# Modulation rows on VectorE from the third group on, in a two-layer hybrid backbone on one Trainium2 core

## The chip, the core and the metric

The kernel runs on one core of a Trainium2 chip. Time is device microseconds (us) of one launch. The profile follows one execution; its engines are called PE or TensorE (matrix products; PEld is its weight load), DVE or VectorE, ACT or ScalarE, POOL or GpSimd, and SP, whose queue issues nearly all transfers from DRAM here. The on-chip memories are SBUF and, for TensorE's results, PSUM.

## The reference

Two layers over 256 latent tokens and 256 context tokens, width 2048, in float32. Cut to what matters here:

```python
for l in range(DEPTH):                                  # DEPTH = 2
    shift, scale, gate = split(silu(c) @ ada_w[l] + ada_b[l], 3)         # and the same with c_ctx
    h  = rmsnorm(x,  norm_g[l]) * (1.0 + scale)   + shift                # modulation
    hc = rmsnorm(xc, norm_g[l]) * (1.0 + scale_c) + shift_c
    q, k, v, up, uf, g = split_proj(h @ w_in[l])        # and the same of hc
    q = rope(rmsnorm(q, q_norm_g[l])); k = rope(rmsnorm(k, k_norm_g[l]))
    att = softmax attention of q over context and latent keys
    out = (concat(att, pool(up), fourier(uf)) * silu(g)) @ w_out[l]
    x = x + gate * out
return rmsnorm(x, final_norm_g)
```

`silu(c) @ ada_w` is a product of two vectors (c and c_ctx) with a 2048 x 6144 matrix in each layer. The parts shift and scale of layer 0, 2048 x 4096 values, have to be there before the first h is.

## The kernel before, in words

Tokens lie along the free axis and channels on the 128 partitions: x is 16 tiles (k = 0 to 15) of 128 channels x 512 tokens, latent and context side by side, held in four SBUF tiles `xk[0..3]` of four k each. The framework that the kernel is written in places waits and buffers by itself: a tile drawn from a pool with so many buffers waits until an earlier tile of it is free. Instructions of each engine, and the transfers on SP's queue, run in order; the order is made ahead of time from priorities and a model of durations. In the startup TensorE's order is the one written in the code (`manual_schedule`, L989).

Every product with large weights is done in a split form: a float32 value is taken apart into a high and a low part (`split`, L137: ScalarE casts, VectorE subtracts), and three passes (high x high, high x low, low x high) are summed in PSUM.

**The startup** (`startup`, L838 to L1055) does four things at once:

- *The norm.* `stats(g)` (L855) squares the four k of one x tile on ScalarE and VectorE and sums them over partitions by a matmul with a matrix of ones (L871). `norm()` (L875) does the last of them, `stats(3)`, then root and reciprocal (L878, L880).
- *The modulation of layer 0.* It goes by ten groups of k, `GROUPS = (1, 1, 2, 2, 2, 2, 2, 2, 1, 1)`. Group j needs shift and scale for its one or two k: 2048 rows of the matrix by 256 or 512 columns, loaded in four pieces of 512 rows (`piece`, L972; 512 KB or 1 MB; the tile is called `a` in the profile, from pool `st` with four buffers). `ada_part` (L979) multiplies one piece by silu(c) and silu(c_ctx): four matmuls on four column strips of the array. After the last piece the sum is copied (L1018), transposed (L1024), reduced (L1031), biased and scaled (L1039, L1040), and `make_h` (L245) makes the h of its k: a product with the norm's reciprocal (L248), scale and shift (L255), split.
- *A quarter of the rows on VectorE.* `ND[j] = 1` gives one of a group's four pieces to VectorE, so that TensorE has three. `dvec` (L952) loads that piece with columns on the partitions and 512 rows along the free axis, and takes for each of c and c_ctx a product with a copy of silu(c) on all partitions and its sum (L965, eight of them for a group of two k). The copies, `cq`, are read from DRAM (L958), where `late["store"]` (L160) put silu(c) after a transpose in group 0. The partial sums are added at L1038. Before the change the groups 5 to 9 are done like this. `dvec(j + 1)` is called in group j, ahead of its last piece.
- *The first matmuls with h.* Weights `wb` (two column blocks) and `wgs` (some gate columns) are loaded and split as jobs (`queue`, L941), and their matmuls go into a list `backlog`; `work(n)` (L924) takes up to n of them, 14 after each piece of a group of two k. An entry is held back until a counter of pieces, `now`, has reached its `ready` value: the h of group j is taken from the second piece of group j + 1 on (`QK = 1`). With fewer TensorE pieces in a group the counter starts the group further on (`kk + 4 - npc`, L1005).

`warm(n)` (L985) issues n small matmuls of ones into a PSUM tile that is not read.

**Loads in program order.** The first 12 k of x (L832), then in group 0 its first piece, the last four k of x (L999), and the other pieces. SP's queue works through this order; a transfer whose buffer is not free, or whose source is not written, holds up those behind it.

**The layers** follow: column blocks of the input projection (`b_chunk`), with small work put between by a side list, `Side` (L258): each entry has a generator, a delay on the list's own clock (a row of main matmuls counts 0.64) and an entry that it must follow. `q_prep` (L518) makes the queries: norm, rotation, and transposes on TensorE (L525); it is put on the list at L648 with a delay of `LAG_E` = 5.6. Meanwhile VectorE works off the rest of the modulation matrix (L188).

Of the kernel before, what the change touches and what calls it, by code (L numbers as in the profile page):

```python
# [20 lines left out]
P = 128  # L21
# [9 lines left out]
AHEAD = 400  # L31
ST = 4
KS = 8
ND = (0, 0, 0, 0, 0, 1, 1, 1, 1, 1)
KG = 4
NE = 3
DLOW = -60
# [9 lines left out]
LAG_S, LAG_T, LAG_E, LAG_Q = 4.3, 1.4, 5.6, 0.0  # L47
GROUPS = (1, 1, 2, 2, 2, 2, 2, 2, 1, 1)
# [8 lines left out]
def backbone(  # L57
# [24 lines left out]
    V, S, G, PE = nc.vector, nc.scalar, nc.gpsimd, nc.tensor  # L82
# [31 lines left out]
    def load_x(g, n):  # L114
        for j in range(0, 4, n):
            nc.sync.dma_start(xk[g][:, j : j + n], xT[:, 4 * g + j : 4 * g + j + n])

    idt = const.tile([P, P], F32, name="idt")
    ones = const.tile([P, P], F32, name="ones")
# [164 lines left out]
    side = Side()  # L284
# [233 lines left out]
    def q_prep(qraw, qT, rq):  # L518
        rq.append(head_rstd(qraw, 4, P ** -0.5))
        for tt, r in qraw:  # L520
            qo = rope_one(tt, r, 4, 0)
            yield 0.0, 3.0 if tt == 0 else 1.0
            tp = smt()
            for hh in range(4):
                PE.transpose(tp[:, hh * P : hh * P + P], qo[:, hh], idt)  # L525
            c = slice(tt * P, tt * P + P)
            split(tp.rearrange("p (h n) -> p h n", h=4), qT[0][:, :, c], qT[1][:, :, c])
            yield 0.43, 0.0
# [47 lines left out]
    def layer(l, h, xs, chunk0):  # L576
# [62 lines left out]
        for g in range(2):  # L639
            accs = b_chunk(l, 3 + g, h, ntt, FILL[l][2])  # L640
            qraw = evac_raw(accs)
            if l == 0:
                side.finish("a0")
                qT = pair8(4, (T,))
            else:
                qT = [a.rearrange("p a (b n) -> p (a b) n", b=2) for a in pair8(2, (2 * N,))]
            rq = []
            side.add(f"q{g}", q_prep(qraw, qT, rq), LAG_E, "k")  # L648
            for qt in range(ntt):
                side.add(f"a{g}", attention(g, qt, qT, rq, kT, vv, mixed, off), 0.0, f"q{g}")  # L650
        korder = list(range(8, 16)) + list(range(8))
# [48 lines left out]
        k = KT - 1  # L700
# [128 lines left out]
            V.scalar_tensor_tensor(th, th, 1.0, g, op0=ALU.add, op1=ALU.mult)  # L829
        return th  # L830

    for g in range(3):  # L832
        load_x(g, 2)
    cq = [f4("cq", (P, 2, 512), F32) for _ in range(2)]
    h0 = H(T, "h")

# [1 line left out]
    def startup():  # L838
        st = tc.tile_pool(name="st", bufs=ST)
        with st as st:  # L840
# [111 lines left out]
            def dvec(j):  # L952
                gs, k0, n = GROUPS[j], sum(GROUPS[:j]), P * GROUPS[j] * 1024
                for e in range(ND[j]):
                    if ND[j - 1] < ND[j] and not used[e]:
                        used[e] = True
                        for v in range(2):
                            nc.sync.dma_start(cq[e][:, v], late["cd"][v, 1536 - 512 * e : 2048 - 512 * e].partition_broadcast(P))  # L958
                    raw = st.tile([P, 2 * gs, 512], F32, tag="a0", name=name("a0"))
                    pi = start[j] + (3 - e) * n  # L960
                    nc.sync.dma_start(raw, ada0[pi : pi + n].rearrange("(p b r) -> p b r", b=2 * gs, r=512))
                    with tc.high_priority(offset=DLOW):
                        for q in range(2 * gs):
                            for v in range(2):
                                V.scalar_tensor_tensor(  # L965
                                    t2("junk") if v == 0 else raw[:, q], raw[:, q], 1.0, cq[e][:, v], op0=ALU.mult, op1=ALU.mult,
                                    accum_out=abq[:, e, q // gs, k0 + q % gs, v : v + 1],
                                )
# [15 lines left out]

            def warm(n):  # L985
                for _ in range(n):
                    PE.matmul(first[3][:, :P], ones, ones, start=True, stop=True)

            with tc.manual_schedule(engines={mybir.EngineType.PE}):  # L989
                for g in range(3):  # L990
                    stats(g)
                for j, gs in enumerate(GROUPS):
                    a = smt()
                    w_ = 256 * gs
                    npc = 4 - ND[j]
                    raws = []
                    for kk in range(npc):
                        if j == 0 and kk == 1:
                            load_x(3, 1)  # L999
                        if j == 1 and kk == 3:  # L1000
                            late["store"]()
                        if kk == npc - 1 and j + 1 < len(GROUPS):
                            dvec(j + 1)
                        raws.append(piece(j, kk))
                        now[0] = 4 * j + kk + 4 - npc  # L1005
                        if kk + 4 - npc == (PFK if j else 3):
                            queue(4 * j + 4 + (QK if j else Q0), k0, gs)
                        if j == 0 and kk == 2:
                            norm()
                        if j == 0 and kk == 3:  # L1010
                            nc.sync.dma_start(idt, ident)
                        ada_part(a, raws[kk], kk, kk == 0, kk == npc - 1, w_)
                        if j == 1 and kk < 2:
                            warm(3 - 2 * kk)
                        work(RATE * gs // 2)
# [167 lines left out]
```

## Time and profile before

| | |
|---|---|
| median of 3 runs | 1073.24 us (1071.56 to 1074.11) |
| the profiled execution | 1073.19 us, span 1071.4 us |
| TensorE busy | 1047.4 us, 98% of the span |
| VectorE busy | 842.3 us, 79% |
| ScalarE busy | 479.7 us, 45% |
| read from DRAM | 230.58 MB |

The span is the part of the execution that the profile covers. Busy time is summed over an engine's instructions. The "chain of waits" follows the run back from its end, at each step to what released it. A row of instructions gives start, length, engine, line, operation, the tiles written and read, and in square brackets how long the engine had idled before and what ended it. A row of a transfer gives the tiles, the issuing queue, the size, and the time from issue to landing.

### The profile page before, as it was taken

To read this page: it belongs to the slowest core of one execution; us is meant where nothing else is said; L and a number is where in the kernel's file an instruction comes from. 1 tells how busy PE (TensorE), PEld (TensorE's weight loads), DVE (VectorE), ACT (ScalarE), POOL (GpSimd) and SP (SyncE) were. 2 spreads that over 40 slices of the span, in tenths; PEclk is the share of its full clock that TensorE was granted. 3 is DMA by queue.
4 is the path that set the end of the run, shared out by engine and by line. 5 is a ranking of instruction groups with operands and counts; after the bars stand their busy time and mean duration, and the time that the engine had idled before them with its cause. 6 is when DMAs were issued, how large, how long until landed. Compare 5 with 4: busy or idle time off the path is not lost.

```text
span 1071.4 us, 14049 instructions
## 1 busy us (share of the span) xinstructions
PE 1047.4 (98%) x5100; PEld 842.6 (79%) x5100; DVE 842.3 (79%) x1553; ACT 479.7 (45%) x803; POOL 0.2 (0%) x4
## 2 busy tenths in 40 slices
PE   6899999999999999999999999999999999999996
PEld 4466677888787888888888888887888888888885
DVE  6358648998999779998989787489657889776565
ACT  5233225323323766632522223288326767447453
POOL 0000000000000000000000000000000000000000
PEclk9999999999999999999999999999999999999999
DMA  8999777566785244457776667445764565686563
GB/s 336 410 398 343 256 238 242 164 198 214 227 260 169 80 140 158 157 192 273 266 272 213 197 195 265 139 133 169 271 218 161 168 196 185 224 270 212 192 201 117
DMA packets 63797, 233.63 MB, mean 218 GB/s; under 512 B 7104, under 2 KB 8176, under 8 KB 60016
## 3 DMA queue, kind: packets, MB, share of 16 engines
q1 hardware_dynamic: 63152, 231.69, 63.8%
q10 hardware_dynamic: 576, 1.05, 0.3%
q8 instruction: 40, 0.66, 0.3%
q14 instruction: 29, 0.24, 0.1%
HBM read 230.58 MB, written 2.12 MB: 217 GB/s over the span
## 4 chain that ended last, share of the span: by engine, by line
PE 81%; DVE 7%; DMA 4%; ACT 3%; issue 3%; SPq 0%; DVEq 0%; ACTq 0%
PE mm L336 18%; PE mm L335 18%; PE mm L337 18%; PE mm L932 6%; PE mm L311 5%; PE sm L932 3%; DVE ajunk L188 2%; DMA a<-in_ada 2%; PE mm L312 2%; PE sm L336 2%; PE sm L337 2%; PE sm L335 2%; PE sm L981 2%; DVE wlo L139 2%; PE sm L562 1%
## 5 line engine op out<-in xcount | busy, mean ns | idle before, releaser
L138 ACT CAST whi<-raw 128x1024 fp32r<-128x1024 f32 (+1 forms) x216 | 219.9, 1019 | 333.0 <-PE mm L336 112.1
L139 DVE TENSOR_TENSOR wlo<-raw,whi 128x1024 fp32r<-128x1024 f32 (+1 forms) x216 | 255.3, 1182 | 103.7 <-ACT whi L138 102.6
L188 DVE SCALAR_TENSOR_TENSOR ajunk<-araw,cbt 128x1024 bf16<-128x1024 f32 x224 | 273.6, 1221 | 49.8 <-DMA araw<-in_adar 36.9
L335 PE MATMUL mm<-whi,h 128*128 128x512 f32 x416 | 167.6, 403 | 0.0
L336 PE MATMUL mm<-wlo,h 128*128 128x512 f32 x416 | 163.3, 393 | 0.0
L337 PE MATMUL mm<-whi,h 128*128 128x512 f32 x416 | 163.1, 392 | 0.0
L335 PE MATMUL mm<-m,whi 128*128 128x512 f32 (+1 forms) x272 | 102.6, 377 | 0.0
L336 PE MATMUL mm<-m,whi 128*128 128x512 f32 (+1 forms) x272 | 102.4, 377 | 0.0
L337 PE MATMUL mm<-m,wlo 128*128 128x512 f32 (+1 forms) x272 | 102.4, 377 | 0.0
L311 PE MATMUL mm<-h,whi 128*128 128x512 f32 x256 | 92.5, 400 | 0.0
L337 PEld LDWEIGHTS mm<-whi,h 128*128 128x128 f32 x416 | 78.1, 188 | 17.0 <-DVE h L139 0.3
L336 PEld LDWEIGHTS mm<-wlo,h 128*128 128x128 f32 x416 | 78.2, 188 | 16.2 <-issue 1.9
L335 PEld LDWEIGHTS mm<-whi,h 128*128 128x128 f32 x416 | 78.2, 188 | 16.1 <-issue 1.7
L335 PE MATMUL mm<-h,whi 128*128 128x512 f32 x196 | 77.7, 396 | 0.0
L337 PE MATMUL mm<-h,wlo 128*128 128x512 f32 x196 | 76.8, 392 | 0.0
L336 PE MATMUL mm<-h,whi 128*128 128x512 f32 x196 | 76.8, 392 | 0.0
L312 PE MATMUL mm<-h,wlo 128*128 128x256 f32 x256 | 72.4, 283 | 0.0
L932 PE MATMUL mm<-whi,h 128*128 128x512 f32 x192 | 63.8, 401 | 0.2 <-ACT h L138 0.2
L335 PEld LDWEIGHTS mm<-m,whi 128*128 128x128 f32 x272 | 51.2, 188 | 9.5
L337 PEld LDWEIGHTS mm<-m,wlo 128*128 128x128 f32 x272 | 51.2, 188 | 9.4
L336 PEld LDWEIGHTS mm<-m,whi 128*128 128x128 f32 x272 | 51.2, 188 | 9.2
L311 PEld LDWEIGHTS mm<-h,whi 128*128 128x128 f32 x256 | 48.1, 188 | 10.8
(229 smaller groups left out, 1639.1 us busy)
## 6 DMA issues: line engine op xcount, KB each, us to landing
araw<-in_adar SPq DMA_DIRECT2D x128, 512.0 KB, 4.0
raw<-in_wb SPq DMA_DIRECT2D x78, 512.0 KB, 3.6
raw<-in_wg SPq DMA_DIRECT2D x55, 512.0 KB, 4.3
a<-in_ada SPq DMA_DIRECT2D x24, 1024.0 KB, 9.1
raw<-in_wo SPq DMA_DIRECT2D x32, 512.0 KB, 4.3
raw<-in_wot SPq DMA_DIRECT2D x32, 512.0 KB, 3.9
a<-in_ada SPq DMA_DIRECT2D x16, 512.0 KB, 4.6
x<-in_xT SPq DMA_DIRECT2D x4, 1024.0 KB, 8.1
```

The lines of the kernel that those rows point to most:

```text
L138: i = S.copy(hi, src)
L139: V.tensor_sub(lo, src, hi.bitcast(F32))
L188: V.scalar_tensor_tensor(junk, raw, 1.0, cbt[:, v], op0=ALU.mult, op1=ALU.mult, accum_out=acc[:, u, h, v : v + 1])
L311: PE.matmul(a.rearrange("p (s n) -> p s n", s=2), hi[:, j - j0], h.both[k][:, :, :N], start=s0, stop=False)
L312: PE.matmul(a[:, :N], lo[:, j - j0], h.hi[k][:, :N], start=False, stop=s1)
L335: PE.matmul(o, ah, bh, start=start, stop=False)
L336: PE.matmul(o, ah, bl, start=False, stop=False)
L337: PE.matmul(o, al, bh, start=False, stop=stop)
L562: PE.transpose(tp[:, h * P : h * P + P], ps[h][:, i * P : i * P + P], idt)
L932: PE.matmul(o, lt, r, start=s0, stop=s1)
L981: PE.matmul(a[32 * i : 32 * i + 32, :w_], cs[:, 4 * kk + i], raw[:, i], start=first_, stop=last, tile_position=(0, 32 * i))
```

## The change

VectorE gets a quarter of the rows in groups 2, 3 and 4 as well. In these groups `dvec` is called in the group itself, after its first piece; from group 5 on it is called in the group before, as it was, but after that group's last piece has been issued, not ahead of it. The store of silu(c) now comes behind the last piece of group 1. All four tiles of x are loaded ahead of the modulation, and the norm stands ahead of group 0 in TensorE's order. Small matmuls of ones are added at the start and between the pieces of group 0, and they write another PSUM tile. In layer 0 `q_prep` gets 1.5 more delay on the side list.

```diff
-ND = (0, 0, 0, 0, 0, 1, 1, 1, 1, 1)
+ND = (0, 0, 1, 1, 1, 1, 1, 1, 1, 1)
...
-            side.add(f"q{g}", q_prep(qraw, qT, rq), LAG_E, "k")
+            side.add(f"q{g}", q_prep(qraw, qT, rq), LAG_E + (1.5 if l == 0 else 0.0), "k")
...
-    for g in range(3):
-        load_x(g, 2)
+    for g in range(4):
+        load_x(g, 2 if g < 3 else 1)
...
-                    if ND[j - 1] < ND[j] and not used[e]:
+                    if not used[e]:
...
-                    PE.matmul(first[3][:, :P], ones, ones, start=True, stop=True)
+                    PE.matmul(gfirst[0][:, :P], ones, ones, start=True, stop=True)
...
             with tc.manual_schedule(engines={mybir.EngineType.PE}):
+                warm(10)
                 for g in range(3):
                     stats(g)
+                norm()
...
                     for kk in range(npc):
-                        if j == 0 and kk == 1:
-                            load_x(3, 1)
+                        raws.append(piece(j, kk))
                         if j == 1 and kk == 3:
                             late["store"]()
-                        if kk == npc - 1 and j + 1 < len(GROUPS):
+                        if kk == 0 and ND[j] and j < 5:
+                            dvec(j)
+                        if kk == npc - 1 and 5 <= j + 1 < len(GROUPS):
                             dvec(j + 1)
-                        raws.append(piece(j, kk))
                         now[0] = 4 * j + kk + 4 - npc
...
-                        if j == 0 and kk == 2:
-                            norm()
...
                         ada_part(a, raws[kk], kk, kk == 0, kk == npc - 1, w_)
+                        if j == 0 and kk < 3:
+                            warm(2)
```

## The prediction

> **What bounds the kernel now.** I read the page first, then the startup in stretches of 10 us, then the chain of waits in order of time, and last single rows.
>
> ```profile
> span 1071.4 us, 14049 instructions
> PE 1047.4 (98%) x5100; PEld 842.6 (79%) x5100; DVE 842.3 (79%) x1553; ACT 479.7 (45%) x803; POOL 0.2 (0%) x4
> ...
> 20.00:30.00 10.00, 9.51 (x76) 5.59 (x68) 7.00 (x16) 3.52 (x8) 0.00 (x0) 1.00 0.87 311
> 30.00:40.00 10.00, 8.77 (x52) 4.75 (x49) 3.10 (x8) 2.76 (x4) 0.00 (x0) 1.00 1.01 423
> 40.00:50.00 10.00, 7.78 (x45) 3.88 (x45) 6.80 (x14) 2.66 (x5) 0.00 (x0) 1.00 1.02 417
> 50.00:60.00 10.00, 10.00 (x51) 6.41 (x50) 2.16 (x3) 2.78 (x5) 0.00 (x0) 1.00 1.02 417
> ```
>
> The columns after the stretch are its length, then busy us and instructions of PE, PEld, DVE, ACT and POOL, the granted clock, the DMA share and GB/s. Over the whole run TensorE is the bound: 24 us of 1071.4 are not busy. The change lies in the startup, and there the picture has two halves. From 30 to 50 us TensorE has holes while the DMA engines are full (423 and 417 GB/s, share above 1.0). From 50 us TensorE is full and the DMA is nearly so. VectorE has room throughout (3.10 to 6.80 us of 10).
>
> ```profile
> 26.66 7.67 DMA a<-in_ada
> ...
> 34.38 1.11 PE sm L981 x8
> ...
> 35.50 11.06 DMA a<-in_ada
> ...
> 46.61 1.06 PE sm L981 x8
> 47.67 3.40 PE mm L932 x14
> 51.07 1.00 PE sm L981 x8
> ...
> 55.47 1.00 PE sm L981 x8
> ```
>
> This is the chain of waits: start, length, what. Up to 46.6 us it is modulation pieces on their way in; after that only TensorE. So an edit that takes TensorE work out before about 46 us buys nothing by itself, and one that takes it out later buys its full length, as long as the transfers still arrive. They only just do:
>
> ```profile
> a<-in_ada SPq DMA_DIRECT2D x1, 1024.0 KB, 12.3
> ...
> 42.73 0.33 SPq L976 DMA_DIRECT2D a<-in_ada  x1
> ```
>
> The fourth piece of group 3 (counting from 0) is issued at 42.73 us and lands 12.3 us later, at 55.0; its matmuls start at about 55.4. The DMA stream is therefore the bound up to 55 us, with 0.4 us to spare.
>
> **The change, part by part.** *A piece less on TensorE in groups 2, 3 and 4.* A modulation piece of 128x512 takes 1.00 us in the chain (51.07), and 14 main matmuls follow it (3.40 us). The three pieces are worth 3 x 1.0 = 3.0 us of TensorE. Group 2 is used up at 32 to 43 us and group 3 up to 55.4 us, both while the transfers are the bound; only group 4's piece lies wholly in the full stretch. I count **-1.0 us** (bounds 0 and -3.0).
>
> *The same rows on VectorE.* Each group adds eight products.
>
> ```profile
> 73.15 0.69 DVE L965 SCALAR_TENSOR_TENSOR junk<-a,cq 128x512 f32<-128x512 f32 x1
> ...
> 77.44 0.69 DVE L965 SCALAR_TENSOR_TENSOR a<-a,cq 128x512 f32<-128x512 f32 x1
> 78.05 0.08 DVE L965 DVE_READ_ACCUMULATOR a<-a,cq 128x1 f32 x1
> 78.05 1.29 DVE L248 TENSOR_TENSOR xn<-x,rstd 128x512 f32<-128x512 f32 x2
> ```
>
> Eight take 78.05 - 73.15 = 4.9 us; three groups 14.7 us, plus three additions of the partial sum (about 0.2 us each). VectorE idles 6.9 us of 30 to 40 and 7.8 us of 50 to 60, so I cost them at nothing. The cover is the time until the last piece of the same group has landed: the VectorE piece lands ahead of two more pieces, each 1 MB, which at 417 GB/s take 2.5 us each, so 5 us against 4.9 us, and evacuation, transposes and reduction come after. If the products were late by 2 us in one group, the next main matmuls would be late by as much. VectorE is in order: behind a product that waits for its piece stand the splits of the weights, the reduction and the h of the group before, and TensorE's main matmuls wait for these. TensorE has about 3 us to spare between 32 and 43 us; I take 0, bounds 0 and +2.
>
> *The copies of c come forward.* Two loads of 256 KB move from 56.9 us to a place between group 2's first and second pieces, into the stretch that the transfers bound.
>
> ```profile
> 56.88 0.91 SPq L958 DMA_DIRECT2D cq<-cd  x2
> ...
> cq<-cd SPq DMA_DIRECT2D x2, 256.0 KB, 10.6
> ```
>
> 0.52 MB at 417 GB/s is **+1.3 us** on all that lands after them. They also wait for the store of c to DRAM, on SP's in-order queue. Behind them stand the VectorE piece, the weight loads and pieces 1 and 2 of group 2.
>
> ```profile
> 24.34 0.38 SPq L160 DMA_DIRECT2D cd<-crow  x1
> 24.77 2.96 SPq L976 DMA_DIRECT2D a<-in_ada  x4
> ...
> cd<-crow SPq DMA_DIRECT2D x1, 16.0 KB, 2.9
> ...
> a<-in_ada SPq DMA_DIRECT2D x1, 512.0 KB, 4.6
> ```
>
> The store landed in 2.9 us on an almost empty queue; a piece issued just after it took 4.6 us. It now goes out after group 1's last piece, at about 25.2 us, so it lands at 28 to 30. Until then group 1's last piece and group 2's first are under way, 1.5 MB or 3.6 us at 417 GB/s. I take no hole, bounds 0 and +6 (the slower rival below). [...]
>
> *x ahead, and the norm ahead of group 0.* The four loads of x's last quarter move past one 512 KB piece, 1.3 us at 417 GB/s. They feed the squares, and those the reciprocals:
>
> ```profile
> 13.52 1.99 ACT L862 ACTIVATE sq<-x 128x512 f32<-128x512 f32 x3 [1.40 <-DVE sq L868]
> ...
> 19.04 3.37 DVE L880 RECIPROCAL rstd<-rstd 128x256 f32<-128x256 f32 x2 [2.05 <-ACT rstd L878]
> ...
> 22.32 0.11 DVE L1031 TENSOR_REDUCE red<-sm 128x4 f32<-128x16 f32 x1
> ...
> 23.16 0.68 DVE L139 TENSOR_TENSOR wlo<-raw,whi 128x512 fp32r<-128x512 f32 x1
> ...
> 20.29 0.94 PE L987 MATMUL mm<-ones 128*128 128x128 f32 x6
> ...
> 20.37 0.43 SPq L145 DMA_DIRECT2D raw<-in_wb  x1
> ...
> 23.91 0.33 SPq L145 DMA_DIRECT2D raw<-in_wgs  x1
> ```
>
> Both reciprocals end at 22.4 us, together with group 0's reduction, which does not move (the same bytes lie ahead of its last piece). But the first weight split stands behind them on VectorE and ends at 23.84; SP waits for it from 20.8 to 23.91, and that hole is the 311 GB/s of 20 to 30 us. ScalarE's squares of the last quarter waited 1.4 us for buffers that VectorE's additions free, and start no sooner, so I let the reciprocals, the split and SP move by 0.8 us of the 1.3: **-0.8 us** on the stream (bounds 0 and -1.3). The ten plus six small warm matmuls (three took 0.94 us at 20.29, two instructions to a matmul) fill TensorE's holes ahead of 24 us and cost nothing: the ten come before the first squares. Without that cover, ten would cost 3.1 us.
>
> *Order.* With three TensorE pieces, the counter that releases a group's main matmuls is one step further on, so group 1's and group 2's h come up after one piece of the next group, not two, and TensorE waits for h there. The rows I followed it by:
>
> ```profile
> 41.60 1.06 PE L981 MATMUL sm<-a,cs 128*32 128x512 f32 x8
> ...
> 44.13 0.19 DVE L1031 TENSOR_REDUCE red<-sm 128x8 f32<-128x32 f32 x1 [1.53 <-PE sm L1024]
> ...
> 46.17 1.34 DVE L139 TENSOR_TENSOR h<-xn,h 128x512 fp32r<-128x512 f32 x2
> ```
>
> The last piece of group 2, used at 41.6 us now, comes at 41.6 + 1.3 - 0.8 + 0.9 = 43.0 us (two weight loads, 0.9 MB, now stand ahead of it; 0.9 is my allowance for them), its reduction 2.5 us later at 45.5 as now, and the first of the two h 2.7 us after that (46.17 + 0.67 - 44.13), so the first main matmul at 48.2, fourteen of them to 51.6, piece 1 to 52.6, fourteen to 56.0. The last TensorE piece of group 3 lands at 55.0 + 1.3 - 0.8 = 55.5, so I put its start near 55.7, about halfway between what the transfers and what this order allow; it is at 55.4 now: **+0.3 us** net for everything before it (it holds the +1.3 and the -0.8).
>
> *A later start of the q preparation in layer 0*, by 1.5 us of the side queue's clock:
>
> ```profile
> 334.84 0.39 PE L337 MATMUL mm<-whi,h 128*128 128x512 f32 x1
> 336.23 0.63 PE L525 MATMUL sm<-idt,qo 128*128 128x128 f32 x4 [1.00 <-DVE nt L235]
> ```
>
> TensorE stands 1.0 us at the first transposes, waiting for VectorE. Three rounds of 0.64 us later that is gone if VectorE's chain ends when it did: **-1.0 us** (bounds 0, if the chain slips along, and -1.0).
>
> **Sum.** +0.3 - 1.0 - 1.0 = -1.7 us. The span goes to 1069.7 us; the profiled execution took 1073.19 us with 1.8 us outside its span and lies on the median of 1073.24, so I forecast 1073.2 - 1.7 = 1071.5 us.
>
> **The rivals.** *TensorE gets all of it.* If the stream has more slack than I give it (the lost hole at 20 to 30 us closes wholly, and 0.4 us spare was no limit), three pieces, the start and the q wait pay: -3.0 - 0.8 - 1.0 = -4.8, **1068.4 us**. For it: TensorE is the only engine in the chain from 46.6 us. Against it: 417 GB/s and a share of 1.02 up to 60 us.
>
> *Nothing moves.* The transfers eat the pieces (last landing +1.3, no gain at the start) and the q chain slips along: +1.3 - 1.0 = +0.3, **1073.5 us**. For it: the bounds of each term; against it: the waits named above have a releaser that does move.
>
> *Slower: SP stands at the copies of c.* If the store is overtaken by nothing and lands as late as a transfer does once the queue is full:
>
> ```profile
> 27.78 0.54 SPq L145 DMA_DIRECT2D raw<-in_wb  x1
> ...
> raw<-in_wb SPq DMA_DIRECT2D x1, 512.0 KB, 10.4
> ```
>
> 10.4 us, then SP is held from 25.6 to 35.6 us, what is under way runs dry at about 31, and the stream loses 4.6 us: -1.7 + 4.6 = +2.9, **1076.1 us**. It decides from a landing of about 7.5 us, at which the hole outweighs the gains. For it: the stream is the bound just there. Against it: what lies ahead of the store then is little (2.9 us now).
>
> **How the numbers follow.** Less than 0.2%, 2.1 us, can't be told from no change here. The forecast gets 0.45; its own range is 1069.8 to 1073.0, and as 1071.1 us is the mark for faster I give 0.18 of it to faster and 0.27 to no change. TensorE gets all of it: 0.24, faster. Nothing moves: 0.13, no change. Slower: 0.18. So faster 0.42, same 0.40, slower 0.18. The range reaches a little below the second case and nearly to the slower one: 1067.3 to 1075.5.
>
> **What would show it.** In the profile after: 24 more products at L965, first between 34 and 42 us, without a wait of VectorE for a piece ahead of them; matmuls at L981 fewer by 3 x 8; the copies of c issued before 30 us, and a DMA rate above 400 GB/s from 28 to 55 us, which shows the slower rival wrong; the last TensorE piece of group 3 at 55 to 56 us (clearly sooner would show the first rival right); both reciprocals over by 21.7 us; no 1 us wait ahead of the first L525 transposes; the last L932 matmul about 0.7 us sooner than now. The prediction is wrong if TensorE's holes before 50 us shrink by several us, or if SP stands at L958 for over 7 us.

## The result, and the profile after

The changed kernel takes 1078.74 us (median of 6 runs, 1077.86 to 1079.26), the kernel before 1073.28 us beside it (6 runs, 1071.56 to 1074.11). The ratio is 1.0054, 95% interval 1.0041 to 1.0066: slower by 5.5 us, 7.2 us above the forecast and outside its range. The profiled execution took 1078.32 us.

First the page of the changed kernel, then its row for 28 to 34 us and its stretches of 10 us, with the columns of the same view of before.

```profile
span 1076.5 us, 14126 instructions
...
PE 1053.6 (98%) x5108; PEld 847.6 (79%) x5108; DVE 857.3 (80%) x1604; ACT 479.8 (45%) x803; POOL 0.2 (0%) x4
...
28.00:34.00 6.00, 5.67 (x38) 3.23 (x41) 2.25 (x6) 1.16 (x3) 0.00 (x0) 1.00 0.68 233
...
30.00:40.00 10.00, 8.24 (x43) 4.66 (x41) 3.23 (x9) 1.50 (x3) 0.00 (x0) 1.00 0.78 308
40.00:50.00 10.00, 6.95 (x25) 2.78 (x26) 8.05 (x20) 2.42 (x3) 0.00 (x0) 0.66 1.02 412
50.00:60.00 10.00, 8.69 (x45) 5.10 (x44) 9.17 (x27) 1.98 (x3) 0.00 (x0) 1.00 1.03 415
```

The same 6 us of before:

```profile
28.00:34.00 6.00, 4.88 (x30) 2.42 (x29) 2.40 (x7) 1.32 (x3) 0.00 (x0) 1.00 1.01 421
```

The bound stretch has lost transfers. From 28 to 34 us the DMA engines moved 233 GB/s at a share of 0.68, where before moved 421 GB/s at 1.01; over 30 to 40 us it is 308 against 423. The stretches behind it run at 412 and 415 GB/s again (before: 417 in both), so what was lost there is not made up. The granted clock, 1.00 throughout this part of before, is 0.66 from 40 to 50 us.

Where the 5.1 us of span lie is read from the row of the startup's last matmuls, and from the first matmul of layer 0's output projection. The last two numbers of a row are the starts of its first and last instruction; before first, then after.

```profile
L932 PE MATMUL sm<-h,wlo x60: 388/389/499, 30.0 to 170.2; 128*128 128x512 f32 x60
...
L336 PE MATMUL mm<-m,whi x272: 280/389/389, 527.5 to 702.6; 128*128 128x512 f32 x120, 128*128 128x256 f32 x16
```

```profile
L932 PE MATMUL sm<-h,wlo x60: 388/389/796, 31.3 to 175.4; 128*128 128x512 f32 x60
...
L336 PE MATMUL mm<-m,whi x272: 280/389/389, 533.8 to 708.9; 128*128 128x512 f32 x120, 128*128 128x256 f32 x16
```

The startup ends 5.2 us later (175.4 against 170.2) and layer 0 as far as its output projection takes 1.1 us more (533.8 - 175.4 = 358.4 against 357.3). All that follows gives back 1.2 us, so the loss stands in the two places that the change touches. "Startup end" below is the last number of this L932 row.

The chain of waits of the changed kernel, and SP's queue as it worked through the same time (start, length, what):

```profile
24.97 4.60 DMA cd<-crow
30.96 11.33 DMA a<-in_ada
42.33 1.93 PE sm L981 x8
44.27 3.29 PE sm L932 x7
47.55 1.56 PE sm L981 x8
```

```profile
24.97 0.42 SPq L160 DMA_DIRECT2D cd<-crow  x1
25.48 0.37 SPq L976 DMA_DIRECT2D a<-in_ada  x1
29.59 0.80 SPq L958 DMA_DIRECT2D cq<-cd  x2
30.48 0.38 SPq L961 DMA_DIRECT2D a<-in_ada  x1
30.96 0.38 SPq L976 DMA_DIRECT2D a<-in_ada  x1
31.43 1.10 SPq L145 DMA_DIRECT2D raw<-in_wb  x1
32.62 1.61 SPq L145 DMA_DIRECT2D raw<-in_wgs  x1
34.28 1.13 SPq L976 DMA_DIRECT2D a<-in_ada  x2
```

The store of c to DRAM landed after 4.60 us, and SP issued nothing from 25.85 to 29.59 us, when it could issue the copies of c. Group 2's second TensorE piece follows at 30.96 and takes 11.33 us to land. TensorE's own rows (in brackets the idle time before and what ended it) show the price, and VectorE's show that it waited too:

```profile
42.33 1.93 PE L981 MATMUL sm<-a,cs 128*32 128x512 f32 x8 [3.01 <-DMA a<-in_ada]
...
47.48 1.58 PE L981 MATMUL sm<-a,cs 128*32 128x512 f32 x8
...
60.86 1.06 PE L981 MATMUL sm<-a,cs 128*32 128x512 f32 x8
...
39.85 0.69 DVE L965 SCALAR_TENSOR_TENSOR junk<-a,cq 128x512 f32<-128x512 f32 x1 [3.60 <-DMA a<-in_ada]
...
44.14 0.69 DVE L965 SCALAR_TENSOR_TENSOR a<-a,cq 128x512 f32<-128x512 f32 x1
...
50.54 0.19 DVE L1033 TENSOR_REDUCE red<-sm 128x8 f32<-128x32 f32 x1 [2.49 <-PE sm L1026]
```

Group 2's last TensorE piece is used at 47.48 us (41.60 before), its reduction comes at 50.54 (44.13 before), and group 3's last piece is used at 60.86 (55.40 before). From there to the startup end TensorE waits only once more, for 0.71 us (below), and the delay stays.

### The profile page after: what moved, and what is told of

Same layout as the page of the kernel before. It is cut to its first block, busy times and chain, and to the rows that moved or that the text cites. A ratio compares the mean times of both kernels' runs of the same rounds, so it can differ in the third digit from the quotient of the medians.

```text
span 1076.5 us, 14126 instructions
## 1 busy us (share of the span) xinstructions
PE 1053.6 (98%) x5108; PEld 847.6 (79%) x5108; DVE 857.3 (80%) x1604; ACT 479.8 (45%) x803; POOL 0.2 (0%) x4
## 4 chain that ended last, share of the span: by engine, by line
PE 81%; DVE 9%; issue 4%; DMA 4%; ACT 1%; SPq 0%; DVEq 0%; ACTq 0%
PE mm L335 17%; PE mm L336 17%; PE mm L337 17%; PE mm L932 6%; PE mm L311 5%; DVE ajunk L188 4%; PE sm L932 3%; PE mm L312 3%; PE sm L981 2%; PE sm L335 2%; PE sm L336 2%; PE sm L337 2%; DVE wlo L139 2%; PE sm L562 2%; DMA a<-in_ada 1%
## 5 line engine op out<-in xcount | busy, mean ns | idle before, releaser
L335 PE MATMUL mm<-whi,h 128*128 128x512 f32 x416 | 167.7, 403 | 0.0
L335 PE MATMUL mm<-m,whi 128*128 128x512 f32 (+1 forms) x272 | 102.6, 377 | 0.0
L335 PEld LDWEIGHTS mm<-whi,h 128*128 128x128 f32 x416 | 78.3, 188 | 15.9 <-issue 1.7
L335 PE MATMUL mm<-h,whi 128*128 128x512 f32 x196 | 77.8, 397 | 0.1
L932 PE MATMUL mm<-whi,h 128*128 128x512 f32 x192 | 63.7, 400 | 1.7 <-ACT h L138 1.7
L335 PEld LDWEIGHTS mm<-m,whi 128*128 128x128 f32 x272 | 51.2, 188 | 9.5
```

Source lines behind the costliest of these rows:

```text
L335: PE.matmul(o, ah, bh, start=start, stop=False)
L932: PE.matmul(o, lt, r, start=s0, stop=s1)
```

## The experiments

Five rounds each. "Piece" is the time at which group 2's last TensorE piece is used, "end" the startup end, both of the one profiled execution; before has 41.6 and 170.2. Ratios are to the kernel before, run beside each.

| run | what | ratio (95%) | piece | end |
|---|---|---|---|---|
| the change | | 1.0054 (1.0041 to 1.0066) | 47.5 | 175.4 |
| e1 | before + later q preparation | 1.0024 (1.0014 to 1.0034) | 41.8 | 170.4 |
| e2 | before + new start | 1.0047 (1.0035 to 1.0059) | 42.7 | 171.6 |
| e3 | the change, old start | 1.0054 (1.0039 to 1.0069) | 45.8 | 173.7 |
| e4 | the change, copies without the wait | 1.0057 (1.0045 to 1.0069) | 45.7 | 174.6 |
| e5 | the change, TensorE kept busy | 1.0081 (1.0066 to 1.0096) | 47.3 | 174.7 |
| e6 | before + VectorE's pieces alone | 1.0033 (1.0023 to 1.0043) | 46.5 | 174.2 |
| e7 | the same from group 4 on | 1.0019 (1.0007 to 1.0030) | 42.1 | 170.5 |
| e8 | e6, copies without the wait | 1.0035 (1.0023 to 1.0047) | 46.2 | 173.6 |
| e9 | e6, copies left out | 1.0003 (0.9992 to 1.0013) | 41.4 | 168.8 |
| e10 | e6, copies from 128 rows | 1.0022 (1.0011 to 1.0033) | 43.3 | 170.8 |
| e11 | e7, saves behind the evacuation | 1.0016 (1.0007 to 1.0024) | 42.6 | 170.9 |
| e12 | e2 without the pairs | 0.9996 (0.9987 to 1.0005) | 42.0 | 170.6 |
| f1 | the change without the pairs | 1.0053 (1.0041 to 1.0066) | 47.6 | 175.0 |
| f2 | the change, copies left out | 1.0016 (1.0007 to 1.0025) | 43.5 | 172.3 |
| f3 | the change without the three causes | 0.9988 (0.9979 to 0.9997) | 41.3 | 169.8 |
| f4 | f3 + c spread by TensorE | 1.0013 (1.0003 to 1.0023) | 43.2 | 170.7 |
| f5 | f4, halves behind groups 0 and 1 | 0.9994 (0.9985 to 1.0003) | 43.3 | 170.8 |
| f6 | e6 + c spread as in f5 | 1.0014 (1.0005 to 1.0023) | 45.3 | 172.8 |

### The parts alone: e1, e2, e3, e6

The first theory was that the copies of c, by their wait or their transfers, make group 2 late; the rivals were the new start and the later q preparation. Each part was put into the kernel before by itself (e3 takes the new start out of the changed kernel).

e1:
```diff
-            side.add(f"q{g}", q_prep(qraw, qT, rq), LAG_E, "k")
+            side.add(f"q{g}", q_prep(qraw, qT, rq), LAG_E + (1.5 if l == 0 else 0.0), "k")
```


> The kernel before with the later q preparation alone. Theory (the wait of 1.0 us ahead of the first L525 transposes goes away, nothing else moves): 1.0 us less than before, 1072.3 us, and no such wait in the trace. Rival (the chain slips along, or a wait of like size comes up elsewhere): 1073.3 us, within 0.3 of before.

e2 (e3 takes these same lines out of the changed kernel):
```diff
-    for g in range(3):
-        load_x(g, 2)
+    for g in range(4):
+        load_x(g, 2 if g < 3 else 1)
...
+                warm(10)
                 for g in range(3):
                     stats(g)
+                norm()
...
-                        if j == 0 and kk == 1:
-                            load_x(3, 1)
...
-                        if j == 0 and kk == 2:
-                            norm()
...
+                        if j == 0 and kk < 3:
+                            warm(2)
```


> The kernel before with the new start alone: all of x ahead, the norm ahead of group 0, the small warm matmuls. Theory start (TensorE takes the pieces of group 0 later, behind the norm and the warm matmuls, so their buffers come free later and group 1's pieces are issued later): first main matmul about 1.9 us later than before as in the changed kernel, 1.0 to 2.0 us slower, 1074.3 to 1075.3. Rival hold (all of the loss comes from SP held at the copies of c): no loss here, 1072.5 to 1073.3.

> The changed kernel with the old start. Theory start: 1.9 us less than the changed kernel, about 1076.8. Rival hold: SP is still held at the copies of c for 3 to 4 us, 1078 to 1079, no more than 0.5 us less than the changed kernel.

e6 is the change without e1's and e2's lines: `ND = (0, 0, 1, 1, ...)`, with `dvec(j)` called behind the first piece of groups 2 to 4.

> The kernel before with the VectorE pieces of groups 2 to 4 alone: old start, old q preparation. By sums: the run with the old start and the new q preparation was 5.0 us over before, and the new q preparation alone 2.5 us, so 2.5 us over before if the two add up. Theory core (the copies of c, two loads of 256 KB ahead of group 2's other pieces, and SP's wait for the store make group 2 end about 4 us later, and only 1.0 us of TensorE comes back): 2.5 to 4 us over before. Rival (nearly all comes from the q preparation and the start): no more than 1 us over before.

All three parts cost something alone, e1 0.24%, e2 0.47%, e6 0.33%; together that is 1.04%, nearly twice the 0.54% of the whole, so they overlap. e1 lost 2.5 us where both of its expectations had no loss; e2 lost 5 us of median where 1 to 2 were expected; and e3, the changed kernel with the old start, is no quicker than the changed kernel (1.0054 both). e6 has the late piece (46.5 us) by itself, with the old start.

e1 shows what became of the q wait. Rows of 345 to 400 us (columns as above), before first, then e1 with the waits of TensorE in it:

```profile
345.00:400.00 55.00, 55.00 (x278) 45.77 (x277) 43.72 (x101) 37.95 (x79) 0.00 (x0) 1.00 0.36 115
```

```profile
345.00:400.00 55.00, 52.71 (x260) 42.23 (x259) 41.36 (x94) 36.28 (x77) 0.00 (x0) 1.00 0.34 114
...
354.62 0.50 PE L335 MATMUL sm<-kh,q 128*128 128x512 f32 x1 [0.55 <-ACT p L545]
...
392.00 0.84 PE L562 MATMUL sm<-idt,p 128*128 128x128 f32 x4 [0.90 <-ACT p L550]
397.86 0.51 PE L336 MATMUL sm<-ptl,vh 128*128 128x512 f32 x1 [0.81 <-DVE ptl L139]
```

The 1.0 us wait at the first L525 transposes is gone, and 2.3 us of new waits stand in the attention that starts later with the queries: TensorE now waits there for ScalarE's probabilities (L545, L550) and VectorE's splits of them. That accounts for 1.3 of the 2.5 us that e1 loses; the rest lies in stretches that count as busy and was not found. The stretch from the startup end to the first matmul of layer 0's output projection shows the cost in every kernel with this line: 358.0 to 360.6 us in the seven profiles with the later q preparation, 356.3 to 357.9 in the thirteen without it. In the changed kernel the larger part of it is no wait: waits at L335 and L562 (0.5 and 0.9 us) replace the 1.0 us, and the same matmuls are busy for 356.0 us instead of 354.9.

### The wait and the clock: e4, e8, e5

Two candidates for what makes group 2 late: SP's wait for the store, and the transfers of the copies themselves; a third is the clock that fell with TensorE's 3 us hole (0.50 from 42 to 48 us, behind a wait of 3.01 us). In e4 (the change) and e8 (e6) the copies read the final norm's weights, an input, so nothing is waited for; the modulation of the groups from 2 on is then computed with other numbers.

```diff
-  nc.sync.dma_start(cq[e][:, v], late["cd"][v, 1536 - 512 * e : 2048 - 512 * e].partition_broadcast(P))
+  nc.sync.dma_start(cq[e][:, v], fgr[0, 1536 - 512 * e : 2048 - 512 * e].partition_broadcast(P))
```


> The changed kernel with the copies of c read from an input of the same size (the final norm's weights) instead of the stored silu(c), so that they wait for no store; the modulation of the groups from 2 on is then computed with other numbers. Bytes, order and instructions are the same. Theory hold (SP is held 3.7 us for the store, the transfers run dry from 30 to 36 us, and TensorE's clock falls in the hole behind it): no wait at L958, the second TensorE piece of group 2 lands 3 to 4 us sooner, TensorE's clock stays at 1.00 from 40 to 50 us, 3 to 5 us less than the changed kernel, 1074 to 1076. Rival bytes (the 0.5 MB of copies and the longer way of the pieces behind them are the cause, whoever waits): within 1 us of the changed kernel, 1078 to 1079.

> The run with the VectorE pieces alone from group 2 on, with the copies of c read from the final norm's weights and not from the store (the modulation of groups 2 on is computed with other numbers). Theory hold (SP's wait for the store costs 1.5 to 2 us of the stream): 1.5 us less than the run with the VectorE pieces alone. Rival bytes (the copies cost their transfer time, wait or not): within 0.5 us of it.

e5 puts 13 matmuls with zeros, summed into a tile in use, ahead of group 2's second TensorE piece:

```diff
+                        if j == 2 and kk == 1:
+                            zero = acc.rearrange("p u h v -> p (u h v)")[:, :P]
+                            for _ in range(13):
+                                PE.matmul(gfirst[0][:, :P], zero, ones, start=False, stop=False)
```


> The changed kernel with 13 small matmuls of zeros, summed into a bank that is in use anyway, ahead of group 2's second TensorE piece, where TensorE stands idle for 3 us and its clock then falls to half for some 7 us. Theory clock (the fall costs about 1 us here by itself: a piece of 1.93 and one of 1.58 us instead of 1.06, and seven matmuls in 3.29 instead of 1.7 us): TensorE's clock stays at 1.00 from 40 to 50 us, 0.5 to 1.5 us less than the changed kernel. Rival (the transfers set the time in that stretch whatever the clock): the clock stays up, the time does not move by more than 0.3 us.

Without the wait the ratio stays where it was (1.0057 against 1.0054; 1.0035 against 1.0033). The piece comes 1.8 us sooner in e4 than in the changed kernel and 0.4 us sooner in e8 than in e6, and the startup ends 0.8 and 0.6 us sooner. The wait is there, but with the copies' transfers still in place taking it away gains no more than that; a kernel with the wait and quick copies was not run.

In e5 the clock is 1.00 in every stretch from 30 to 60 us and the startup ends 0.7 us sooner than in the changed kernel, but the run as a whole is slower still (1.0081): layer 0 up to its output projection takes 360.6 us instead of 358.4, with a wait of 1.8 us at L409 that the changed kernel does not have, and why was not found. So the fall of the clock is worth 0.7 us by this one profile, and not shown by the time. Elsewhere the clock goes with more: in e7 the seven executions with a mean clock of 0.997 or 0.998 took 1071.5 to 1073.6 us, the five at 0.994 to 0.996 took 1075.4 to 1076.8. In the changed kernel no such order is seen (1078.3 us at 0.993, 1079.2 at 0.997). What the fall costs stays open.

### The transfers: e9, e10

e9 leaves the copies out (VectorE multiplies by a constant). e10 keeps two loads of the same size at the same place in the queue, but each partition reads a row of its own from a weight matrix. In both the modulation is computed with other numbers. The edit of e10:

```diff
-  nc.sync.dma_start(cq[e][:, v], late["cd"][v, 1536 - 512 * e : 2048 - 512 * e].partition_broadcast(P))
+  nc.sync.dma_start(cq[e][:, v], wb[0, 0, 0][:, v])
```


> The VectorE pieces of groups 2 to 4 alone, with the copies of c left out: VectorE multiplies by a constant instead of c, so the modulation of groups 2 to 4 and of all later groups is computed with other numbers. Theory (the two copies of c, their wait and their transfers, are what makes the pieces late): the last TensorE piece of group 2 is used at 41.6 to 43 us instead of 46.5, the DMA rate from 28 to 36 us is back above 400 GB/s, the last main matmul of the startup comes at 170.2 to 171.2 us instead of 174.2, median 1072 to 1073. Rival (the order of three pieces and the products on VectorE set the time, whatever is transferred): that piece stays after 45 us, the startup ends after 173 us, median about 1075.

> As e8, but each partition reads its own 2 KB row of a weight matrix instead of all 128 reading the same 2 KB (the same bytes, packets, place in the queue, and no wait; the modulation is computed with other numbers). Theory (128 reads of one address are slow): the DMA rate from 28 to 34 us rises from 304, 309 and 206 GB/s to above 400, group 2's last TensorE piece is used at 42.8 to 43.5 us (41.6 + 0.52 MB at 417 GB/s), the startup ends at 171 to 172 us, median about 1073. Rival (any two loads of 256 KB at this place cost that much): rate as in e8, that piece at about 46 us, startup end at 173.6, median about 1075.8.

The same 6 us in e8 (128 partitions read one row of 2 KB) and in e10 (128 rows), in this order:

```profile
28.00:34.00 6.00, 3.78 (x25) 2.21 (x27) 2.40 (x7) 1.38 (x3) 0.00 (x0) 1.00 0.97 273
```

```profile
28.00:34.00 6.00, 4.45 (x29) 2.06 (x27) 2.39 (x7) 1.29 (x3) 0.00 (x0) 1.00 1.03 409
```

The engines are about as busy in the one as in the other (0.97 and 1.03) and move 273 against 409 GB/s: here the 128 reads of one row are slow, they are not waiting. Other profiles with reads of one row and busy engines agree: 306 GB/s in e4 from 28 to 34 us (share 0.99), and over 30 to 40 us 315 in e5 (1.00), where e10 has 415 (1.02).

Without the copies the difference to before can't be told (1.0003 against 1.0033 with them, about 3.2 us), so they are what VectorE's pieces cost. How these microseconds split is less sure. Through the startup end, e6 to e8 to e10 to e9 (174.2, 173.6, 170.8, 168.8), it would be 0.6 for the wait, 2.8 for reading one row, and 2.0 for the bytes and their place. But these are single executions, e6's 1.1 us above its median and e9's 2.2 below; the granted clock from 40 to 50 us was 0.66 and 0.83 in those of e6 and e8 and 1.00 in those of e10 and e9; and the intervals of e8 and e10 overlap. The low rate is shown; what it costs by itself is not.

The share of 0.97 is a mean over the core's 16 DMA engines, so the low rate does not come from engines that stand idle. What causes it no run here separates further (e10 reads another tensor, too).

### The gain that went: e7, e11

> As the run with the VectorE pieces alone, but from group 4 on, so one group more than before: the copies of c are loaded after group 4's first piece, when group 3's pieces are already on their way. Theory (the transfers stop being the bound at about 55 us, and a TensorE piece taken out after that is worth its 1.0 us): 1.0 us less than before, no wait of SP at the copies. Rival (VectorE's products or the copies hold up group 4 as well): same as before or up to 1 us slower.

e7 (`ND = (0, 0, 0, 0, 1, 1, ...)`) has one TensorE piece less, in group 4, after the bound stretch. The startup should end 1.0 us sooner and ends at 170.5. A new wait stands in its place, here and in every run that has VectorE take a piece of group 4: first ScalarE's rows in the changed kernel, then TensorE's row that waits for them.

```profile
94.83 2.63 ACT L922 COPY part<-mm 128x512 f32<-128x512 f32 x4 [3.77 <-PE mm L932]
97.35 0.59 ACT L1020 COPY ev<-sm 128x512 f32<-128x512 f32 x1
...
98.00 0.66 PE L1026 MATMUL sm<-idt,ev 128*128 128x128 f32 x4 [0.71 <-ACT ev L1020]
```

With three pieces in the groups before, the four copies of the partial products (`save`, L922) come ahead of group 5's evacuation in ScalarE's order. They wait for the last of their matmuls, which starts at 96.4 us, while the evacuation's input had been ready since TensorE was through with the piece at 93.0. TensorE idles 0.71 us. In before the fourth copy comes behind the evacuation and TensorE doesn't wait:

```profile
92.00 0.59 ACT L1018 COPY ev<-sm 128x512 f32<-128x512 f32 x1 [0.67 <-PE sm L981]
92.63 0.59 ACT L922 COPY part<-mm 128x512 f32<-128x512 f32 x1
```

With group 3's last piece 0.5 us later in e7 than in before (55.9 against 55.4), that is the gain of one piece. Why the median lies 1.4 us above before's is not explained by it. e11 was to put the copies behind it:

```diff
-                        save(part, first)
+                        held.append((part, first))
...
                         S.copy(ev[:, :w_], a[:, :w_])
+                        while held:
+                            save(*held.pop())
```


> As e7 (VectorE from group 4 on), with ScalarE's four copies of the partial products issued behind the next group's evacuation instead of ahead of it. Theory (the evacuation of group 5 stands behind these copies on ScalarE, and that wait ate the gain of the piece less): the 0.6 to 0.7 us wait of TensorE for the evacuation at 97 us is gone, the last main matmul of the startup comes 0.9 to 1.2 us sooner than in e7 (169.3 to 169.6 us), median 0.5 to 1.0 us under the kernel before. Rival (another wait takes its place): 170.2 us or later, median as e7, 1 us over the kernel before.

It did not change what it was meant to change: in its trace the four copies still run first (at 90.33 us, the evacuation at 92.86), since ScalarE's order is made ahead of time by priorities and not by the order of the lines; it is no quicker (1.0016). That the copies' place causes the wait is read from the rows, not shown by taking it away; that stays open.

### The pairs of small matmuls: e12

> As e2 (x ahead, the norm ahead of group 0), without the pairs of small matmuls between group 0's pieces. Theory (the pairs delay the freeing of group 0's buffers, and so group 1's pieces): the first main matmul comes at 24.7 us instead of 26.2, the startup ends at 170.2 us, median as the kernel before. Rival (the norm's matmuls ahead of the pieces delay them): first main matmul after 26 us, startup end at 171.6, median 2 to 5 us over the kernel before.

The edit is e2 without its last two lines. Group 0's pieces on TensorE in e2, then in e12, with the first main matmul of each:

```profile
17.35 0.64 PE L981 MATMUL sm<-a,cs 128*32 128x256 f32 x8
...
20.98 0.64 PE L981 MATMUL sm<-a,cs 128*32 128x256 f32 x8
...
26.22 0.48 PE L932 MATMUL mm<-whi,h 128*128 128x512 f32 x1
```

```profile
17.42 1.50 PE L981 MATMUL sm<-a,cs 128*32 128x256 f32 x24
19.58 0.64 PE L981 MATMUL sm<-a,cs 128*32 128x256 f32 x8 [0.66 <-DMA a<-in_ada]
...
25.36 0.48 PE L932 MATMUL mm<-whi,h 128*128 128x512 f32 x1
```

Three pieces had landed by the time the norm was through (one row, 24 instructions), so there were no holes for the pairs to fill: each pair put 0.64 us between two pieces, and group 0's last one came 1.4 us later (20.98 against 19.58). Without the pairs the new start makes no difference (0.9996). The first main matmul is still 0.7 us later than before's 24.66, so the rival of the expectation has a part in it, without effect on the time. The medians of e2 and e12 differ by 5.0 us, but their startup ends by 1.0: the profiled e2 is the shortest of its runs, and where the others lose more is not seen.

### Taken away from the changed kernel: f1, f2, f3

> The changed kernel without the pairs of small matmuls between group 0's pieces. Theory (each cause costs by itself): as e12 against e2, 5 us less, median about 1073.7. Rival (the late start of group 1 lies behind the copies of c, which then make group 2's last piece late anyway): as e3, about 1 us less, median 1077.5, with group 2's last TensorE piece still used after 45.5 us.

> The changed kernel with the copies of c left out; VectorE multiplies by a constant, so the modulation is computed with other numbers. Theory (each cause costs by itself): 2 to 3 us less, as e9 against e6, median about 1076. Rival (the copies are the one that bounds the startup of the changed kernel): group 2's last TensorE piece back at 43 us, startup end at 171 to 172 us instead of 175.4, median about 1074.5.

> The changed kernel without the three causes: no pairs of small matmuls, no copies of c (VectorE multiplies by a constant, so the modulation is computed with other numbers), q preparation at its old time. What is left is VectorE's pieces, x ahead and the norm ahead. Theory (the three causes are the whole): 1072.5 to 1073.4, as e9 and e12, no difference to the kernel before that can be told. Rival (something else in the new start with the new pieces costs too): 1074.5 or more.

Edits as in e12, in e9, and both together with e1's line undone. The rival expectations came nearest for f1 and f2. Without the pairs the changed kernel is no quicker (1.0053, piece at 47.6 us); not even the 1 us that the rival gave it shows. Without the copies it goes from 1.0054 to 1.0016, about 4 us, and the rate is back:

```profile
30.00:40.00 10.00, 8.91 (x49) 4.76 (x49) 7.44 (x23) 2.26 (x4) 0.00 (x0) 1.00 1.01 414
```

So the copies bound the changed kernel and hide the pairs' delay; once they are gone the pairs and the later q preparation are what is left (f2 to f3, 0.28%). Through the startup end: 175.4, 172.3 without the copies, 169.8 without the pairs too (in f2's profiled execution, 2.1 us above its median, the granted clock was 0.73 from 40 to 50 us and 0.93 from 50 to 60, so a part of its 172.3 may be that). f3 computes the modulation with other numbers, as e9 does; it is the only variant under the kernel before, by 0.12% (0.9988, 0.9979 to 0.9997), with the 0.71 us wait of e7 still in it.

### A version without the transfers: f4, f5, f6

> As f3, with c spread over the partitions by TensorE instead of left out: VectorE makes two diagonal blocks from c, two matmuls with a block of ones sum them over the partitions, ScalarE copies the sums; no transfer, no wait for the store, everything computed. Theory (the transfers of c are what costs): within 0.5 us of f3, 1072.5 to 1073.9. Rival (the two matmuls, about 2 us, and two more copies come into the way of group 1's evacuation): 1 to 2 us over f3, median about 1075.

> As f4, with one of the two sums over the partitions behind group 0 and the other behind group 1, each at the end of its group. Theory (f4's loss over f3 is the two waits for ScalarE's copy of the first sum): these waits are gone, the last main matmul of the startup 0.7 to 1.2 us sooner than in f4, median 1072 to 1072.7, within 0.2% of the kernel before. Rival (any work put into groups 0 and 1 delays their evacuation): first main matmul later than 25.6 us, median 1073.7 or more.

> VectorE's pieces of groups 2 to 4 alone (old start, old q preparation), with c spread by TensorE as in f5. Theory (as f5): as e9 without the copies, 1072.5 to 1073.5, startup end at 168.5 to 170 us. Rival (with the old start VectorE is in the reciprocals when the first diagonal block is due, and group 0's h comes later by its 0.7 us): first main matmul at 25.2 us or later, startup end after 170.5 us, median 1074 or more.

Everything is computed here; c is spread by a matmul of ones with a diagonal block (f5; f4 does both halves behind group 1, f6 is f5 with the old start):

```diff
+                        if j < 2:
+                            V.tensor_mul(
+                                cq[0][:, j].rearrange("p (k n) -> p k n", n=P), idt.unsqueeze(1).to_broadcast([P, 4, P]),
+                                cvk[:, j, 12:16].unsqueeze(2).to_broadcast([P, 4, P]),
+                            )
+                            PE.matmul(a, ones, cq[0][:, j], start=True, stop=True)
+                            S.copy(cq[0][:, j], a)
```

f4 gives back what f3 had won (1.0013), as its rival had it. TensorE waits twice for ScalarE's copies of the sums in the middle of the bound stretch:

```profile
34.02 1.13 PE L1040 MATMUL sm<-cq,ones 128*128 128x512 f32 x2 [0.67 <-ACT cq L1041]
35.83 1.07 PE L980 MATMUL sm<-a,cs 128*32 128x512 f32 x8 [0.68 <-ACT cq L1041]
```

f5 is at 0.9994, no difference to before. Its median came out as the theory had it, but its profile does not show the theory's reason: a wait of 0.67 us for ScalarE's copy is still there (36.09 us), the startup ends at 170.8 us, as f4's does, and the first main matmul is at 27.1 us, as its rival had it. f6 went the way of its rival (1.0014, startup end 172.8). No version beats the kernel before by what could be told, beyond f3, which leaves the copies out.

## Why the prediction was wrong, by its steps

*Copies of c forward, +1.3 us: the step that failed most.* They were priced by their bytes at the stream's rate. Leaving them out shows what they cost: by the medians about 4 us in the changed kernel (f2) and about 3.2 us in e6 (e9). That the stretch with their 128 reads of one row ran at 273 GB/s, and at 409 with 128 rows, is the part of the reason that the runs show (e8, e10). Before's trace had a hint: its copies, issued at 56.88 us, sit ahead of a stretch of 2 us at a full share and a low rate,

```profile
64.00:66.00 2.00, 2.00 (x10) 1.66 (x9) 1.34 (x2) 0.99 (x2) 0.00 (x0) 1.00 1.00 333
```

but by that row (2 x (417 - 333) GB/s = 0.17 MB, 0.4 us) the price would still have been put too low. There the copies ran among several other transfers.

*The wait for the store, 0.* "I take no hole" was wrong: SP was held from 25.85 to 29.59 us, and the DMA share of 0.68 from 28 to 34 us is a hole. Still the value was about right: taking the wait away gains 0.6 to 0.8 us of startup and nothing that can be told of the time (e4, e8). The slower rival came nearest in time (1076.1 us), but its mechanism, SP at L958, is not the one; it asked for a landing of 7.5 us and the store took 4.60. SP did not stand at L958 for over 7 us, one of the listed signs of being wrong, and the prediction was wrong all the same.

*x and the norm ahead, -0.8, and the warm matmuls at nothing.* The reciprocals did come sooner, and bought nothing.

```profile
17.22 3.37 DVE L880 RECIPROCAL rstd<-rstd 128x256 f32<-128x256 f32 x2 [1.30 <-ACT rstd L878]
...
23.26 0.17 DVE L1033 TENSOR_REDUCE red<-sm 128x4 f32<-128x16 f32 x1 [1.88 <-ACT crow L157]
23.35 0.68 DVE L139 TENSOR_TENSOR wlo<-raw,whi 128x512 fp32r<-128x512 f32 x1
```

They are over by 20.6 us instead of 22.4, within the 21.7 that the prediction gave; but group 0's reduction slipped to 23.26 (22.32 before), and the split behind it starts at 23.35 (23.16 before), so SP's hole did not close. The assumption that they "fill TensorE's holes" failed for the six matmuls between the pieces: with the norm ahead the pieces had landed and there were no holes (e12). Without these no gain is seen either: the startup ends at 170.6 us against 170.2, and the ratio of 0.9996 (0.9987 to 1.0005) cannot tell 0 from -0.8.

*Later q preparation, -1.0.* The wait went as predicted; the term's sign was wrong, the second step that failed. It counted only whether VectorE's chain would slip, not what starts later with it. Alone it costs 2.5 us; in the changed kernel layer 0's first part is 1.1 us longer instead of 1.0 shorter. New waits are a part of that; why the same matmuls are busy for 1.1 us longer stays open.

*A piece less on TensorE, -1.0.* The step was right on its own (products of 4.9 us, hidden; 24 more of them; 24 fewer matmuls at L981), but the new order on ScalarE put a wait of 0.71 us behind it (e7). The prediction followed VectorE and SP past the moved work, not ScalarE.

*The products on VectorE, 0.* Right: the last of group 2's eight starts at 44.14 us and TensorE's last piece is used at 47.48. The 3.60 us wait ahead of the first one, at 39.85, which was not to be there, is the transfers' doing.

*Order: group 2's last piece at 43.0 us, group 3's at 55.7.* They came at 47.5 and 60.9; without the copies alone at 43.5 and 57.8 (f2, with a granted clock of 0.73 from 40 to 50 us), without the pairs too at 41.3 and 55.2 (f3). So the order itself was followed rightly, and what made it late was not in it. Of the signs listed, the copies were issued before 30 us (29.59), but the rate above 400 GB/s from 28 to 55 us, which was to go with it, is the sign that failed first.

Along the two profiles, in the prediction's own terms: up to group 3's last piece it came to +5.5 us where +0.3 stood (the copies, the start and the order). From there to the startup end it is -0.3 instead of the -1.0 of a piece less, with the 0.71 us wait in between. Layer 0 up to its output projection is +1.1 instead of -1.0. What follows gives back 1.2 us, which was not forecast and which no run explains. Together that is 5.1 us of span where -1.7 stood. How the first 5.5 us divide between the copies and the start can't be said, as the two overlap (f1).

## What to carry to other kernels

Price a transfer that is moved into a stretch bound by transfers by a rate that its own access pattern has shown, not by its bytes: here the stretch with one row read by all partitions ran at 273 GB/s (e8), with loads of that size from 128 rows at 409 (e10). When the work of a group becomes shorter, look at every engine's order behind it, and when a wait is removed by starting later, follow what starts later with it. And take each suspect away from the changed kernel too, not only add it to the old one: the costs here overlap, and alone they add up to nearly twice the whole.

## What the hardware showed

In a stretch of 6 us with two loads of 256 KB whose 128 partitions read the same 2 KB, the rate was 273 GB/s at a share of 0.97 (e8); with the same loads from 128 different rows it was 409 at 1.03 (e10).

The granted clock fell after a hole of TensorE of about 3 us in some runs and not in others. In the changed kernel a wait of 3.01 us was followed by 0.50 from 42 to 48 us; f1 waited 3.10 us at the same place and kept 1.00:

```profile
42.81 1.06 PE L981 MATMUL sm<-a,cs 128*32 128x512 f32 x8 [3.10 <-DMA a<-in_ada]
...
42.00:44.00 2.00, 1.19 (x9) 0.35 (x10) 2.00 (x7) 0.00 (x0) 0.00 (x0) 1.00 1.03 432
```

What decides between the two is not shown. A single long hole was not needed either: in e4 the clock was 0.84 from 40 to 50 us, behind waits of 1.13, 1.81, 0.70 and 0.35 us, and in f2 0.73, behind 1.89, 0.71 and 0.35; the piece that followed took 1.93 us in both, where the one before took 1.07 and 1.06. In e10 a wait of 2.16 us went with a clock of 1.00 over the same 10 us.
